# Attention in a two-layer encoder trunk: the value projection in four 256-feature passes between the q/k projections, one head per slot

## The chip, the cores and the metric

The kernel runs on one core of one Trainium2 chip. TensorE multiplies matrices into eight banks of PSUM; VectorE, ScalarE and GpSimd work on SBUF and (the first two) on PSUM; SyncE (SP) issues the loads. The engines run side by side and meet through semaphores; each takes its own instructions in the order in which they are written. The metric is the time of one execution in microseconds, lower is better.

## The reference

The trunk has two layers over 512 positions of 1024 features. Layer 0 is a gated linear attention and an MLP, layer 1 a softmax attention and an MLP; a conditioning vector scales and shifts in front of each. The change is in layer 1's attention, 16 heads of 64 features. Cut to that:

```python
def chunk_attention(u, w_in, b_in, rel_bias, w_out):
    q, k, v = jnp.split(u @ w_in + b_in, 3, axis=-1)
    ...
    # per chunk of 64 queries, over its own chunk and the 8 before it
    s = einsum('bhtd,bhjd->bhtj', qi / 8, kb) + bias
    p = softmax(where(valid, s, -1e30), axis=-1)
    o = einsum('bhtj,bhjd->bhtd', p, vb)
    ...
    return o @ w_out
```

The softmax weights of a query sum to one, so a bias that is added to every value row comes out as the same bias on every output row.

## The kernel before

All matrices are multiplied in pairs of rounded parts: an operand is split into a high part (a cast on ScalarE, the tiles `whi`, `fhi`, and index 0 of an activation tile) and a low part (operand minus high part on VectorE, `wlo`, `flo`, index 1; `lo_of`, L93), and `mm3` (L96) adds three products. A weight unit is 128 x 1024 numbers, 512 KB: a load on SP, a cast on ScalarE, a subtraction on VectorE (on GpSimd for a unit of kind "p"), then 24 products of 512 columns. The list `plan` (from L227) holds the units in the order of use, and `fill(n)` (L179) issues the next loads and splits until n units are ready. Units of kind "e" keep their two parts in the pool of activations rather than in that of weights.

Layer 1's attention is `att` (L852). Before it, the boundary has already projected q and k of pairs 0 and 1. A pair is two heads, since 128 features hold two.

- `vpass` (L968) projects the values, 512 features at a time, in four units and four PSUM banks; VectorE adds the value bias `bv` while it evicts to `vt`. Two passes run first, with scores of heads 0 and 1 between their units (L991, L992).
- Per head: `s_pre` loads a table of relative biases. `s_mm` makes transposed scores, eight products in three banks. `s_a` (L890) adds the biases on VectorE (the part beyond 256 queries is copied by ScalarE), forms maxima over the four key tiles and has GpSimd reduce them over partitions (`partition_all_reduce`, tile `mb`). `s_b1` subtracts `mb` on VectorE, `s_b2` takes exp on ScalarE. `pv` multiplies with values and with ones, so that one bank holds weighted sums and weight totals.
- Per pair: `fin1` (ScalarE: copies of the totals, Ln, Exp of minus it), `fin2` (VectorE: one Newton step, then the products), `fin3` (cast and low part of the result).
- Per q or k unit: `evac_qk` (L826) evicts with scale and bias on ScalarE (tile `f`), then casts on ScalarE (four for q, two for k) and two low parts on VectorE.

The loop `for p in range(6)` (L994) does, per turn, a q and a k unit, scores of two heads, parts of the softmax of both and of the head before, two `pv` and the division of the pair before, in an order written out by hand: `s_b1` of one head stands behind `s_a` of the next, and the ScalarE and VectorE halves of an eviction (`q_hi`, `q_lo`, `k_hi`, `k_lo`) stand apart. The last heads run in `t1` to `t5`, between parts of the first four tiles of the output projection (`ev`, L1079: (tile, k-steps)). Then comes the boundary that normalizes and opens the MLP.

Each engine's order is the order of the calls: the wrapper `InOrder` (L38) chains them.

## Time and profile before

| | us |
|---|---|
| median of 3 runs | 1256.69 (1256.31 to 1257.55) |
| the profiled execution | 1256.22 |
| its span | 1254.5 |
| TensorE busy | 1190.3 (95%) |
| VectorE busy | 884.1 (70%) |
| ScalarE busy | 523.0 (42%) |
| GpSimd busy | 263.3 (21%) |

Busy shares are means over stages with different limits. The value passes lie between about 641 and 690 us, the pair loop between 690 and 796, the last heads and the first output tiles between 796 and 856. In the order-of-time views a row is a run of like instructions: start, length, what it is, how many, and in brackets how long its engine was idle before and what ended that. PEclk is the granted clock of TensorE as a share of 2.4 GHz.

### The profile page before, as it was taken

The page shows a single profiled execution, that of the slowest core. Times are in us where ns is not written, and L with a number is a line of the kernel's source. Part 1 is how long each engine was busy: PE and PEld are TensorE (multiplying, and loading weights), DVE is VectorE, ACT ScalarE, POOL GpSimd, SP SyncE. Part 2 cuts the span into 40 slices and gives each one's busy share as a digit, 9 for nine tenths or more (in the row PEclk, how much of TensorE's full clock was granted, in tenths as well). Part 3 has the DMA queues.
Part 4 walks back from the last instruction along what each step waited for, and adds up shares of the span by engine and source line. Part 5 has one row for each costly group of instructions (what it writes and reads, how often), then busy time and mean ns, then how long its engine had stood idle before and what let it go on. Part 6 is the DMA issues. An engine that isn't in the chain of part 4 may idle for free.

```text
span 1254.5 us, 15345 instructions
## 1 busy us (share of the span) xinstructions
PE 1190.3 (95%) x5834; PEld 994.3 (79%) x5834; DVE 884.1 (70%) x1359; ACT 523.0 (42%) x816; POOL 263.3 (21%) x227
## 2 busy tenths in 40 slices
PE   8898999899999999999899999888999999999995
PEld 5676887898888888888888866667888888888885
DVE  7899889787666576567866798998875443443467
ACT  3243445366233142233483565663662331422424
POOL 4553321730000000004531221225400000000025
PEclk9998899899999999999999999998999999999998
DMA  8744634205666656654034021223055332232202
GB/s 305 269 157 152 234 101 139 97 18 178 196 188 208 189 183 201 185 168 160 8 93 136 17 67 59 68 68 118 18 171 182 96 106 89 95 101 86 99 18 67
DMA packets 48201, 159.62 MB, mean 127 GB/s; under 512 B 5440, under 2 KB 9792, under 8 KB 48128
## 3 DMA queue, kind: packets, MB, share of 16 engines
q1 hardware_dynamic: 48128, 158.66, 39.0%
q8 instruction: 45, 0.74, 0.2%
q14 instruction: 28, 0.23, 0.1%
HBM read 156.54 MB, written 2.10 MB: 126 GB/s over the span
## 4 chain that ended last, share of the span: by engine, by line
PE 54%; DVE 23%; issue 11%; ACT 6%; POOL 4%; DMA 1%; SPq 0%; ACTq 0%; DVEq 0%; POOLq 0%
PE ps L46 54%; DVE af L46 8%; DVE raw L46 3%; DVE x L46 3%; DVE ar L46 2%; ACT af L46 2%; ACT ar L46 2%; POOL af L46 1%; POOL x L46 1%; DVE wlo L46 1%; DVE u L46 1%; ACT whi L46 1%; DVE mods L46 1%; DVE d L46 1%; DMA raw<-ada 1%
## 5 line engine op out<-in xcount | busy, mean ns | idle before, releaser
L46 PE MATMUL ps<-ar,whi 128*128 128x512 f32 (+1 forms) x2816 | 806.6, 375 | 12.8 <-ACT whi L46 6.2
L46 PEld LDWEIGHTS ps<-ar,whi 128*128 128x128 f32 x2816 | 516.7, 191 | 110.1 <-ACT whi L46 9.1
L46 PE MATMUL ps<-ar,wlo 128*128 128x512 f32 (+1 forms) x1408 | 515.7, 373 | 0.5 <-DVE wlo L46 0.4
L46 PEld LDWEIGHTS ps<-ar,wlo 128*128 128x128 f32 x1408 | 268.2, 191 | 47.9 <-DVE wlo L46 2.1
L46 ACT CAST whi<-raw 128x1024 fp32r<-128x1024 f32 (+1 forms) x183 | 183.8, 1013 | 248.7 <-PE ps L46 227.6
L46 DVE TENSOR_TENSOR wlo<-raw,whi 128x1024 fp32r<-128x1024 f32 x154 | 195.5, 1274 | 26.2 <-ACT whi L46 23.8
L46 POOL TENSOR_TENSOR x<-x,af 128x512 f32<-128x512 f32 x14 | 24.7, 1792 | 633.2 <-ACT af L46 633.2
L46 DVE SCALAR_TENSOR_TENSOR x<-ps,mods,x 128x512 f32<-128x512 f32 (+1 forms) x96 | 63.1, 658 | 133.7 <-PE ps L46 133.7
L46 DVE SCALAR_TENSOR_TENSOR raw<-raw,csil 128x1024 f32<-128x1024 f32 x96 | 123.9, 1291 | 5.7 <-DMA raw<-ada 5.7
L46 DVE TENSOR_TENSOR h<-r 128x512 f32<-128x512 f32 (+1 forms) x72 | 49.3, 689 | 88.1 <-ACT r L46 86.9
L46 PE MATMUL ps<-ar,fhi 128*128 128x256 f32 (+1 forms) x448 | 93.9, 307 | 9.7 <-DVE ar L46 8.7
L46 ACT ACTIVATE r<-ps 128x512 f32<-128x512 f32 (+1 forms) x72 | 39.0, 547 | 137.1 <-PE ps L46 137.1
L46 PEld LDWEIGHTS ps<-ar,fhi 128*128 128x128 f32 x448 | 73.4, 194 | 14.2 <-DVE ar L46 10.2
L46 POOL TENSOR_TENSOR wlo<-raw,whi 128x1024 fp32r<-128x1024 f32 x22 | 60.5, 2752 | 98.9 <-ACT whi L46 93.7
L46 PE MATMUL ps<-whi,ar 128*128 128x512 f32 x256 | 80.9, 391 | 0.2 <-ACT whi L46 0.2
L46 DVE TENSOR_TENSOR ar<-h,ar 128x512 fp32r<-128x512 f32 (+1 forms) x72 | 45.6, 633 | 39.5 <-ACT ar L46 38.4
L46 PE MATMUL ps<-ar,flo 128*128 128x256 f32 (+1 forms) x224 | 67.8, 303 | 0.0
L46 ACT CAST ar<-h 128x512 fp32r<-128x512 f32 (+1 forms) x72 | 41.2, 572 | 51.9 <-DVE h L46 51.9
L46 POOL PARTITION_ALL_REDUCE mb<-af x16 | 33.2, 2077 | 133.8 <-DVE af L46 133.8
L46 PEld LDWEIGHTS ps<-whi,ar 128*128 128x128 f32 x256 | 48.1, 188 | 10.6 <-ACT whi L46 0.6
L46 PE MATMUL ps<-wlo,ar 128*128 128x512 f32 x128 | 50.1, 391 | 0.8 <-DVE wlo L46 0.8
L46 ACT ACTIVATE af<-x 128x256 f32<-128x256 f32 (+1 forms) x48 | 22.7, 486 | 56.0 <-POOL af L46 31.5
(140 smaller groups left out, 1147.3 us busy)
## 6 DMA issues: line engine op xcount, KB each, us to landing
raw<-f SPq DMA_DIRECT2D x128, 512.0 KB, 3.5
raw<-ada SPq DMA_DIRECT2D x96, 512.0 KB, 4.4
raw<-a_qk SPq DMA_DIRECT2D x16, 512.0 KB, 3.6
raw<-w_v SPq DMA_DIRECT2D x8, 512.0 KB, 4.3
raw<-w_g SPq DMA_DIRECT2D x8, 512.0 KB, 3.8
raw<-w_go SPq DMA_DIRECT2D x8, 512.0 KB, 4.6
raw<-a_v SPq DMA_DIRECT2D x8, 512.0 KB, 3.5
raw<-a_o SPq DMA_DIRECT2D x8, 512.0 KB, 3.4
```

The lines of the kernel that those rows point to most:

```text
L46: r = f(*a, **k)
```

## The change

1. The value projection becomes four passes of 256 features, two units each (`v_unit`): products of 256 columns, two PSUM banks, four 128 x 256 copies by ScalarE after the second unit. The host packs the weights accordingly (`quarter`).
2. The 20 units stand in one list, `DENSE`: v0 (two units), q2, k2, v1 (two), q3, k3, q4, k4, v2 (two), q5, k5, q6, k6, q7, k7, v3 (two). The first runs alone.
3. Heads 0 to 14 get a slot each: `s_mm`, `s_a`, the first half of the division where a pair is due, one unit, the rest of the division, `s_b`, the result's split, the unit's eviction, and `pv` of the head before (heads 0 to 11). So slot 0 has the second unit of v0, 1 q2, 2 k2 and the first of v1, 3 the second of v1, 4 q3, 5 k3 and q4, 6 k4, 7 and 8 v2, 9 q5, k5 and q6, 10 k6, 11 q7, 12 k7, 13 and 14 v3. The division of pair p is in slot 2p + 3. Head 15, `pv` of heads 12 to 15 and the last two divisions stand between parts of the output projection.
4. The value bias is no longer loaded as a 128 x 1024 tile; it lies in `col` and is added where the divided result is split (`fin3`).
5. Smaller ones: the first 128 maxima are copied by ScalarE; the division has four instructions on VectorE instead of five, three of them fused; the narrow subtraction comes before the 256-wide one; value units are all split on VectorE; two output units instead of four go to the activation pool; the table is loaded one head ahead.

```diff
-    add_units([a_v[k] for k in range(2)], kind="p")
-    add_units([a_v[k] for k in range(2, 8)])
-    for p in range(2, 8):
-        add_units([a_qk[p], a_qk[8 + p]])
+    DENSE = [("v", 0), ("q", 2), ("v", 1), ("q", 3), ("q", 4), ("v", 2), ("q", 5), ("q", 6), ("q", 7), ("v", 3)]
+    for what, i in DENSE:
+        add_units([a_v[2 * i], a_v[2 * i + 1]] if what == "v" else [a_qk[i], a_qk[8 + i]])
...
-            mx = sB[:, 1, :]
-            V.tensor_copy(mx[:, 0:P], s[0][:, 0:P])
+                if j == 0:
+                    A.copy(out=mx[:, 0:P], in_=s[0][:, 0:P])
...
             tt(V, s, s, y, ALU.mult)
-            V.tensor_scalar(out=s, in0=s, scalar1=-1.0, scalar2=2.0, op0=ALU.mult, op1=ALU.add)
-            tt(V, y, y, s, ALU.mult)
-            tt(V, s[0:64, :], pa[0:64, :], y[0:64, :], ALU.mult)
-            tt(V, s[64:128, :], pb[64:128, :], y[64:128, :], ALU.mult)
+            stt(y, s, 2.0, y, ALU.subtract, ALU.mult)
+            stt(s[0:64, :], pa[0:64, :], -1.0, y[0:64, :], ALU.mult, ALU.mult)
+            stt(s[64:128, :], pb[64:128, :], -1.0, y[64:128, :], ALU.mult, ALU.mult)
...
-            A.copy(out=r[:, 0, :], in_=s)
-            lo_of(V, r[:, 1, :], s, r[:, 0, :])
+            bv = col[:, C_BV + p:C_BV + p + 1]
+            A.activation(out=r[:, 0, :], in_=s, func=AF.Identity, bias=bv)
+            stt(r[:, 1, :], s, bv, r[:, 0, :].bitcast(F32), ALU.add, ALU.subtract)
...
+        def v_unit(n, j):
+            if j == 0:
+                vps[n] = [bank(), bank()]
+            w = next_w(False)
+            for kk in range(4):
+                k = 4 * j + kk
+                for i in range(4):
+                    mm3(vps[n][i // 2][:, (i % 2) * HT:(i % 2 + 1) * HT], uk(u, k, i * P, (i + 1) * P), wk(w, kk, HT),
+                        k == 0 and i % 2 == 0, k == KT - 1 and i % 2 == 1)
...
+            def evac():
+                for i in range(4):
...
+                    A.copy(out=ov, in_=vps[n][i // 2][:, (i % 2) * HT:(i % 2 + 1) * HT].rearrange(
...
+        def slot(i, n, pvh=None, first=True):
+            s_mm(i)
+            s_a(i)
+            if i < 15:
+                s_pre(i + 1)
+            f = todo.pop("fin", None)
+            if f is not None:
+                fin1(f)
+            ev = unit() if n else None
+            fill(2)
+            if f is not None:
+                fin2(f)
+            s_b(i)
+            if f is not None:
+                fin3(f)
+            if ev:
+                ev()
+            if pvh is not None:
+                pv(pvh)
+                if pvh % 2:
+                    todo["fin"] = pvh // 2
+            for _ in range(n - 1):
+                ev = unit()
+                fill(2)
+                ev()
...
+        more = {2: 2, 5: 2, 9: 3}
+        for i in range(15):
+            slot(i, more.get(i, 1), i - 1 if 0 < i < 13 else None)
...
+        ev = [e(lambda: s_mm(15), lambda: s_a(15), lambda: fill(2)), (0, range(5)), lambda: pv(12), (0, (5,)),
+              e(lambda: s_b(15), lambda: fill(2)), (1, range(3)), lambda: pv(13), (1, range(3, 6)),
+              e(lambda: fin1(6), lambda: fill(3), lambda: fin2(6)), (2, range(3)), lambda: pv(14), (2, range(3, 6)), lambda: fin3(6),
+              lambda: pv(15), (3, range(6)),
+              e(lambda: fin1(7), lambda: fin2(7), lambda: fin3(7)),
+              (0, (6,)), (1, (6,)), (2, (6,)), (3, (6,)),
+              (0, (7,)), (1, (7,)), (2, (7,)), (3, (7,))]
```

VectorE, from the scores of one head on. In the pair loop before (`ng` marks the score instructions of `s_a`, the last three of four here, `mb` the subtractions of `s_b1`, `ar<-f` the low parts of q or k):

```order
L46 SCALAR_TENSOR_TENSOR af_5829<-ps_5918,ng,af_5830 128x256
L46 SCALAR_TENSOR_TENSOR af_5830<-ps_5919,ng,af_5830 128x256
L46 SCALAR_TENSOR_TENSOR af_5829<-ps_5919,ng,af_5830 128x128
L46 COPY af_5830<-af_5829 128x128
L46 TENSOR_TENSOR af_5830<-af_5829 128x384
L46 TENSOR_TENSOR af_5830<-af_5830 128x256
L46 TENSOR_TENSOR af_5830<-af_5830,af_5829 128x128
L46 TENSOR_TENSOR af_5826<-af_5826,mb_5876 128x512
L46 TENSOR_TENSOR af_5826<-af_5826,mb_5876 128x384
L46 TENSOR_TENSOR af_5827<-af_5827,mb_5876 128x256
L46 TENSOR_TENSOR af_5826<-af_5826,mb_5876 128x128
L46 TENSOR_TENSOR ar_5930<-f_5928,ar_5930 64x512 x2
```

In slot 4 and the start of slot 5 after the change:

```order
L47 SCALAR_TENSOR_TENSOR af_5713<-ps_5798,ng,af_5713 128x256
L47 SCALAR_TENSOR_TENSOR af_5807<-ps_5798,ng,af_5713 128x128
L47 TENSOR_TENSOR af_5713<-af_5807 128x384
L47 TENSOR_TENSOR af_5713<-af_5713 128x256
L47 TENSOR_TENSOR af_5713<-af_5713,af_5807 128x128
L47 TENSOR_TENSOR wlo_5850<-raw_5847,whi_5849 128x1024
L47 TENSOR_TENSOR af_5807<-af_5807,mb_5818 128x512
L47 TENSOR_TENSOR af_5807<-af_5807,mb_5818 128x384
L47 TENSOR_TENSOR af_5807<-af_5807,mb_5818 128x128
L47 TENSOR_TENSOR af_5713<-af_5713,mb_5818 128x256
L47 TENSOR_TENSOR ar_5862<-f_5859,ar_5861 64x512 x2
L47 SCALAR_TENSOR_TENSOR af_5887<-ps_5876,ng,af_5820 128x256
```

Before, the subtractions behind a head's maxima are those of another head (`af_5826` against `af_5829`); after, they are those of the same head (`af_5807`), with one weight split between, and the low parts of the unit stand between them and the next head's scores.

ScalarE, one turn of the pair loop before, from the weight cast to the division (`f` is the eviction of a q or k unit, `af_6000` the division):

```order
L46 CAST whi_5882<-raw_5880 128x1024
L46 CAST ar_5859<-f_5857 64x512 x4
L46 ACTIVATE f_5928<-ps_5892,col 128x512
L46 COPY af_5829<-ps_5917 128x256
L46 COPY af_5829<-ps_5918 128x128
L46 CAST ar_5930<-f_5928 64x512 x2
L46 CAST whi_5953<-raw_5951 128x1024
L46 ACTIVATE af_5826<-af_5826 128x1024
L46 ACTIVATE af_5827<-af_5827 128x256
L46 COPY af_6000<-ps_5959 64x512
L46 COPY af_6000<-ps_5964 64x512
L46 ACTIVATE af_6000<-af_6000 128x512 x2
```

Slot 5 after the change, from the score copies on:

```order
L47 COPY af_5887<-ps_5876 128x256
L47 COPY af_5820<-af_5887 128x128
L47 COPY af_5887<-ps_5877 128x128
L47 COPY af_5902<-ps_5791 64x512
L47 COPY af_5902<-ps_5871 64x512
L47 ACTIVATE af_5902<-af_5902 128x512 x2
L47 CAST whi_5934<-raw_5932 128x1024
L47 ACTIVATE af_5887<-af_5887 128x1024
L47 ACTIVATE af_5820<-af_5820 128x256
L47 ACTIVATE ar_5948<-af_5902,col 128x512
L47 ACTIVATE f_5951<-ps_5907,col 128x512
L47 CAST ar_5953<-f_5951 64x512 x2
```

Before, eviction passes and casts stand ahead of a head's exp (the two ACTIVATE of 128x1024 and 128x256) and the division behind it; after, the division and the weight cast stand ahead of exp, and the result's split, the eviction and the casts behind it.

## Rows read from the trace of the kernel before

**Rows 1.** Busy time by stretch: pair loop (columns: us, PE, PEld, DVE, ACT, POOL, PEclk, DMA).
```profile
690.00:796.00 106.00, 98.53 (x425) 76.38 (x424) 90.61 (x173) 65.47 (x111) 25.26 (x20) 0.98 0.16 50
```

**Rows 2.** Order of time, VectorE (columns: start us, us, work, count, idle before, releaser).
```profile
652.53 2.36 DVE L46 TENSOR_TENSOR wlo<-raw,whi 128x1024 fp32r<-128x1024 f32 x2 [0.63 <-ACT whi L46]
...
716.97 1.53 DVE L46 SCALAR_TENSOR_TENSOR af<-ps,ng,af 128x256 f32<-128x256 f32 x4
...
720.37 1.79 DVE L46 TENSOR_TENSOR wlo<-raw,whi 128x1024 fp32r<-128x1024 f32 x1 [0.49 <-ACT whi L46]
...
726.35 2.54 DVE L46 TENSOR_TENSOR af<-af,mb 128x512 f32<-128x512 f32 x4
...
728.91 1.41 DVE L46 TENSOR_TENSOR ar<-f,ar 64x512 fp32r<-64x512 f32 x2
...
730.35 1.23 DVE L46 TENSOR_TENSOR wlo<-raw,whi 128x1024 fp32r<-128x1024 f32 x1
...
732.85 0.69 DVE L46 TENSOR_TENSOR af<-af 128x512 f32<-128x512 f32 x1 [1.27 <-ACT af L46]
...
736.27 1.70 DVE L46 TENSOR_TENSOR af<-af,mb 128x512 f32<-128x512 f32 x4
...
737.89 0.68 DVE L46 TENSOR_TENSOR ar<-af,ar 128x512 fp32r<-128x512 f32 x1
...
738.61 1.53 DVE L46 SCALAR_TENSOR_TENSOR af<-ps,ng,af 128x256 f32<-128x256 f32 x4
...
822.89 1.51 DVE L46 SCALAR_TENSOR_TENSOR af<-ps,ng,af 128x256 f32<-128x256 f32 x4
...
845.36 3.50 DVE L46 TENSOR_TENSOR wlo<-raw,whi 128x1024 fp32r<-128x1024 f32 x3
...
855.55 3.24 DVE L46 TENSOR_TENSOR flo<-raw,fhi 128x1024 fp32r<-128x1024 f32 x2
```

**Rows 3.** Order of time, TensorE, one turn of the loop.
```profile
702.46 4.48 PE L46 MATMUL ps<-af,vt 128*128 128x512 f32 x16
...
706.69 0.71 PE L46 MATMUL ps<-ar,whi 128*128 128x512 f32 x2
...
712.24 1.44 PE L46 MATMUL ps<-ar,ar 128*128 128x512 f32 x8
```

**Rows 4.** Order of time, ScalarE, the same period.
```profile
728.92 1.37 ACT L46 ACTIVATE af<-af 128x1024 f32<-128x1024 f32 x2 [1.99 <-DVE af L46]
...
730.31 1.18 ACT L46 COPY af<-ps 64x512 f32<-64x512 f32 x2
...
732.72 0.67 ACT L46 ACTIVATE f<-ps,bq 128x512 f32<-128x512 f32 x1
...
736.33 0.62 ACT L46 CAST ar<-af 128x512 fp32r<-128x512 f32 x1 [2.93 <-DVE af L46]
...
739.12 0.66 ACT L46 COPY af<-ps 128x256 f32<-128x256 f32 x2 [2.17 <-DVE af L46]
...
740.94 1.03 ACT L46 CAST whi<-raw 128x1024 fp32r<-128x1024 f32 x1
...
741.88 2.53 ACT L46 CAST ar<-f 64x512 fp32r<-64x512 f32 x4
```

**Rows 5.** Order of time, GpSimd, the same period.
```profile
720.05 1.78 POOL L46 PARTITION_ALL_REDUCE mb<-af  x1 [11.87 <-DVE af L46]
...
726.52 2.15 POOL L46 PARTITION_ALL_REDUCE mb<-af  x1 [4.69 <-DVE af L46]
```

**Rows 6.** A wait of TensorE, and busy time by stretch around it (granted clock: third from last).
```profile
773.02 1.63 PE L46 MATMUL ps<-ar,ar 128*128 128x512 f32 x8 [2.25 <-DVE ar L46]
...
772.00:776.00 4.00, 2.98 (x12) 2.62 (x13) 2.75 (x4) 3.70 (x7) 1.04 (x2) 0.79 0.04 9
...
776.00:780.00 4.00, 4.00 (x15) 3.18 (x15) 3.65 (x6) 1.12 (x3) 0.00 (x0) 0.79 0.41 122
...
780.00:784.00 4.00, 4.00 (x20) 3.04 (x19) 3.97 (x11) 1.75 (x5) 0.00 (x0) 1.00 0.00 0
```

More of the change, by code (lines that the diff above doesn't have):

```diff
@@ L33 @@
 C_BK = 180
-N_COL = 188
+C_BV = 188
+N_COL = 196
 SH1, SC1, G1, SH2, SC2, G2 = range(6)
@@ L58, in trunk @@
 @with_exitstack
-def trunk(ctx, tc, xT, c, ada, cols, gk1, gk2, w_qk, w_v, w_g, w_go, a_qk, a_v, a_bv, a_tab,
+def trunk(ctx, tc, xT, c, ada, cols, gk1, gk2, w_qk, w_v, w_g, w_go, a_qk, a_v, a_tab,
           a_win, a_o, f1, f2, out):
@@ L210, in add_out @@
         for i, u in enumerate(units):
-            plan.append(("e" if early and i < 4 else "p" if i < pool else "w", u))
+            plan.append(("e" if early and 1 < i < 4 else "p" if i < pool else "w", u))
             if fgs and not early and 1 < i < 6:
@@ L982, in both @@
-        def both(*fs):
+        vps = {}
+        def v_unit(n, j):
[7 more added lines that the diff above has]
+                        k == 0 and i % 2 == 0, k == KT - 1 and i % 2 == 1)
+            if j == 0:
+                return lambda: None
+            def evac():
+                for i in range(4):
+                    ov = vt[i][:, 2 * n:2 * n + 2, :].rearrange("p a (b c) -> p a b c", c=64)[:, :, 0:3:2, :]
+                    A.copy(out=ov, in_=vps[n][i // 2][:, (i % 2) * HT:(i % 2 + 1) * HT].rearrange(
+                        "p (a b c) -> p a b c", b=2, c=64))
+            return evac
@@ new lines, in qk_unit, with evac, unit @@
+        def qk_unit(p, is_k):
+            ps = mtile(u, False)
+            def evac():
+                for f in evac_qk(p, is_k, ps):
+                    f()
+            return evac
+        dense = []
+        for what, i in DENSE:
+            for j in range(2):
+                dense.append((v_unit if what == "v" else qk_unit, i, j))
+        def unit():
+            f, i, j = dense.pop(0)
+            fill(1)
+            return f(i, j)
+        todo = {}
+        def slot(i, n, pvh=None, first=True):
[23 more added lines that the diff above has]
+                ev()
@@ L983, in f, with e @@
+        s_pre(0)
+        fill(2)
+        unit()()
+        fill(2)
+        more = {2: 2, 5: 2, 9: 3}
+        for i in range(15):
+            slot(i, more.get(i, 1), i - 1 if 0 < i < 13 else None)
+        def e(*fs):
             def f():
@@ L1153, in half, with quarter @@
         return w.reshape(4, 2, P, 2, S).transpose(3, 0, 2, 1, 4).reshape(8, P, 2 * S)
+    def quarter(w):
+        return w.reshape(2, 4, P, 4, HT).transpose(3, 0, 2, 1, 4).reshape(8, P, 4 * HT)
     colsT = lambda v: v.reshape(-1, P).T
@@ L1174 @@
         "a_qk": mt(aw[:, :2 * D]),
-        "a_v": half(aw[:, 2 * D:]),
-        "a_bv": a["att_b_in"][:, 2 * D:],
+        "a_v": quarter(aw[:, 2 * D:]),
         "a_tab": tab[:, 256][None, :],
```

130 lines of the change are left out of this document (12 added, 118 removed).

## The prediction

> **What bounds the kernel now.** I read the page's busy shares first, then the stretches by engine, then VectorE, ScalarE and GpSimd in order of time through one period of the pair loop, and last TensorE. TensorE is nearly always busy over the whole program, but not in the part that the change rewrites: in the pair loop it works 98.5 of 106 us, VectorE 90.6, ScalarE 65.5 [rows 1]. So no engine is full there. In order of time one finds why: one period is 716.97 to 738.61, 21.64 us for two heads and two projection units [rows 2]. TensorE needs 5.55 us for a unit (706.69 to 712.24), 1.44 for the scores of a head and 4.23 for two heads' weighted sums (702.46 to 706.69), so 2 x 5.55 + 2 x 1.44 + 4.23 = 18.2 [rows 3]. The remaining 3.4 us are a chain that goes back and forth between VectorE and ScalarE, each waiting for the other in its written order: ScalarE is idle 1.99 and 2.17 us for VectorE, VectorE 0.49 and 1.27 for ScalarE [rows 2, 4]. The pair loop hides one thing well: the all-reduce of one head's maxima on GpSimd (1.78 to 2.15 us, [rows 5]) runs while VectorE does another head's work. What a rewrite of this loop is worth is therefore read from its longest in-order chain, not from busy time.
>
> **The change, part by part.** Durations are of one execution of 1256.2 us (span 1254.5, 1.7 around it), 0.5 under the median of the runs; the sum is made against 1256.2.
>
> *Fewer or moved instructions.* The copy of the first 128 maxima leaves VectorE for ScalarE, the division loses one VectorE instruction per pair, the eight evictions of the values leave VectorE for sixteen on ScalarE, two lower halves of value weights come from GpSimd to VectorE. That is some 8 us less of VectorE work. None of it counts by itself; it counts where it stands in a chain below. The value products have half as many columns each and twice the number; I price a value unit like any unit (same columns), bounded above by twice that, and neither reaches the sum, since TensorE is not what a slot waits for.
>
> *The chain of a head without a division (even slots).* VectorE's new order is: scores of head i, one lower half of weights, the four subtractions of head i, the lower halves of the unit's q or k, scores of head i+1. ScalarE's is: score copies, weight cast, exp of head i, bias pass of the unit, casts. Both are strict, so from one head's first score instruction to the next:
> - scores, hand-over and all-reduce: 716.97 to 720.05 + 1.78 = 4.86, less 0.1 for the copy that left, 4.8 with the hop [rows 2, 5]. Before, another head's subtractions lay here; now only one 1.23 us weight instruction does, inside it.
> - subtractions until exp may start: four take 1.70 when GpSimd is quiet (2.54 beside an all-reduce, 726.35); the last, narrower one is not waited for: 1.3.
> - exp 1.4, bias pass 0.7, first cast 0.6 (a quarter of 2.53), two lower halves 1.4 [rows 2, 4].
>
> Sum 10.2 us with a k unit; with a q unit the second lower half waits for the third cast, 10.8. TensorE's own work in that slot is 5.55 + 1.44 + 2.1 = 9.1, so the chain decides.
>
> *The chain of a head with a division (odd slots from 3).* ScalarE: three score copies 1.0 (the second waits for VectorE's first score instruction), the four division steps 730.31 to 732.85 = 2.5, weight cast 1.0. VectorE's weight instruction stands before the division and waits for that cast, though nothing in the division needs it: 1.2. Then division 2.9 (732.85 to 736.27 = 3.4, less the instruction that goes, 0.5), subtractions 1.3, exp 1.4, cast of the result 0.6, bias pass 0.7, cast 0.6, lower halves 1.4. Sum 14.6 with k, 15.2 with q [rows 2, 4].
>
> *Slots with a value unit.* The eviction is ScalarE's, four copies, estimated at 0.35 each from the 0.66 of two score copies [rows 4]. Odd: the chain ends with the result's lower half, 1.0 + 2.5 + 1.0 + 1.2 + 2.9 + 1.3 + 1.4 + 0.6 + 0.7 = 12.6. Even: VectorE is free early, but the next head's maxima wait for ScalarE's copies, which stand behind exp (ends at 7.5) and eviction (8.9); that makes 8.4.
>
> *Slots with more units.* Each further q or k unit adds a weight cast 1.0, a bias pass 0.7 and its casts behind the last ones on ScalarE, then a lower half. Slot 2: the k casts end at 9.4, weight cast 1.0, VectorE's part 1.2, 11.6. Slot 5: k casts end at 13.8, then 1.0 + 0.7 + three q casts 1.9 + 0.7 = 18.1. Slot 9: q casts end at 15.1, the k unit's at 15.1 + 1.0 + 0.7 + 1.3 = 18.1, then 1.0 + 0.7 + 1.9 + 0.7 = 22.4.
>
> *Sum to the last head's scores.* Slots 6, 10, 12 (k): 30.6. 1, 4 (q): 21.6. 2: 11.6. 0, 8, 14 (value): 25.2. 3, 7, 13 (value, odd): 37.8. 11: 15.2. 5: 18.1. 9: 22.4. Together 182.5, and 0.1 per slot for hand-overs, 184. The start is earlier than before: slot 0 comes after one value unit and not after three. Its first score instruction follows the first weight instruction of 652.53 [rows 2], with two ScalarE passes more ahead of it: 654.5, between 653 and 656. So the scores of head 15 come at 654.5 + 184 = 838.5; before, at 822.89 [rows 2]: 15.6 us late.
>
> *The end of the stage.* From there TensorE sets the pace: four weighted sums (8.5) and 27 of the 32 k-steps of the first four output tiles at 0.69 = 18.7, so 27.2. It starts when the last value eviction is done, about 0.5 after the scores. The update of the fourth tile follows 0.9 later: 838.5 + 0.5 + 27.2 + 0.9 = 867.1. Before it ended at 855.55: 11.5 late. Then three weight instructions stand on VectorE (row of 845.36: 3.50) that before had been done in front of the tile updates, and the next row, the lower halves of 855.55, comes after them: the boundary's VectorE chain shifts by 3.5 more [rows 2]. Total +15, 1256.2 + 15 = 1271.
>
> *Hidden costs.* The 512 KB broadcast load of the value bias goes, the small columns grow; both lie under transfers nobody waits for. The two output weights that leave the activation pool free space there only. Loads of score tables now stand one head ahead of their use between the weight loads on SP; a slot of 10 us covers them, and what is queued behind, a weight load, has five buffers. I price both at 0, up to +3 if a slot's table arrives late.
>
> *A price that could come on top.* TensorE will wait in every slot, for score banks or exp. After its wait of 2.25 us at 773.02 the granted clock of 772 to 780 was 0.79, 1.2 GHz for some of it [rows 6]: 8 x 0.21 = 1.7 us lost. In the slots this is hidden (a unit is ready some 10 us before its bias pass). On the path are slots 2 and 9 and the start of the end stage. The Trainium skill (TensorE: Matmul & The Clock Gate, "A second HAM failure mode: psum-queue depth-cycling") describes such small waits between groups as a lasting loss through falling and rising clock; by it every wait costs, while the pair loop here, with several such waits, kept a mean of 0.98 [rows 1]. I take 0 for the clock in the sum and give it a case of its own below.
>
> **Rivals.**
> - *Faster: the slots overlap and cost only their busiest engine.* For: VectorE loses work and the value pass, where it was idle, is spread over all heads. Slot by slot the larger of TensorE's and VectorE's own work sums to about 157 instead of 184, the stage ends 27 us earlier than I say: 1244. It decides if the mean slot is under about 11.2 us instead of 12.3 (15 us over 15 slots is 1 us each). Against: the next head's scores stand behind this unit's lower halves on VectorE, and those behind exp on ScalarE; nothing lets them pass.
> - *No change: chains 1 us a slot shorter than the rows say.* Would need each all-reduce almost hidden; 1256.
> - *The clock stays low.* Four falls on the path (slots 2 and 9, the start and a second wait in the end stage) at 1.7 each: 1271 + 7 = 1278; if half of the 27.2 us of the end stage ran at 1.2 GHz, 1285. For: a wait in each slot, and the fall after the one of 773.02. Against: full clock in 780 to 784 right after the fall [rows 6].
>
> **How the numbers follow.** Forecast (chains as summed, 1262 to 1280): 0.68, time 1271. Clock: 0.16. Faster: 0.11. No change: 0.05. About 0.2% (2.5 us) is what a measurement of this kernel can tell from none. So faster 0.11, same 0.05, slower 0.84. The range leaves out the faster case and the far end of the clock: 1257 to 1285. Its width: each chain is uncertain by 0.4 us a slot, 6 in all; the value unit, tables and first start by 3 each way; the clock by +7.
>
> **What would show it.** Right: in order of time VectorE idles about 2 us before the subtractions in the slots with no division, with the all-reduce as releaser or nothing but GpSimd running, and about 1.8 us before the weight instruction in the others, released by ScalarE's weight cast; even slots of 10 to 11 us, odd ones of 12 to 15; TensorE's busy share from 650 to 840 under 88%; the chain of waits there holds VectorE, ScalarE and GpSimd and almost no TensorE; the scores of head 15 at about 838. Wrong: slots near 9 us; TensorE on the chain inside the slots; a slot waiting for a table or a weight load; or a boundary after the stage that is no later than the stage itself.

## The result: 30 us slower, twice the forecast

The changed kernel takes 1286.76 us (median of 4 runs, 1285.19 to 1287.07), the kernel before 1256.83 beside it: ratio 1.0235, 95% interval 1.0218 to 1.0253. 1271 was forecast, 1257 to 1285 as range. The direction was right, the size half of what came; the profiled execution took 1287.07.

**The stretch as a whole.** Busy time by stretch of the kernel after, columns as in [rows 1]:

```profile
690.00:796.00 106.00, 89.11 (x427) 72.25 (x426) 69.93 (x129) 59.13 (x106) 21.65 (x16) 0.94 0.20 69
650.00:840.00 190.00, 160.06 (x834) 133.11 (x833) 123.78 (x234) 106.14 (x191) 37.90 (x31) 0.94 0.20 64
```

Every engine is busy for less of the same 106 us than before: TensorE 89 for 98.5, VectorE 70 for 90.6. Much the same work is spread over more time, which fits a chain of waits; the row alone does not show one. TensorE's share from 650 to 840 is 84%. The chain that ended last can be followed back to 795.45, and from there to 846.66 it holds work of VectorE, ScalarE and GpSimd and none of TensorE.

**One even and one odd slot.** Order of time on VectorE, head 6 (731.39) and head 7 (742.50), then head 8 (the rows that [rows 2] show of before from 716.97 to 738.61):

```profile
731.39 1.53 DVE L47 SCALAR_TENSOR_TENSOR af<-ps,ng,af 128x256 f32<-128x256 f32 x4
...
734.08 1.22 DVE L47 TENSOR_TENSOR wlo<-raw,whi 128x1024 fp32r<-128x1024 f32 x1
736.98 1.70 DVE L47 TENSOR_TENSOR af<-af,mb 128x512 f32<-128x512 f32 x4 [1.68 <-POOL mb L47]
741.06 1.41 DVE L47 TENSOR_TENSOR ar<-f,ar 64x512 fp32r<-64x512 f32 x2 [2.38 <-ACT ar L47]
742.50 1.53 DVE L47 SCALAR_TENSOR_TENSOR af<-ps,ng,af 128x256 f32<-128x256 f32 x4
...
747.37 1.23 DVE L47 TENSOR_TENSOR wlo<-raw,whi 128x1024 fp32r<-128x1024 f32 x1 [2.09 <-ACT whi L47]
...
754.78 0.75 DVE L47 SCALAR_TENSOR_TENSOR ar<-af,col,ar 128x512 fp32r<-128x512 f32 x1 [1.71 <-ACT ar L47]
```

The waits named ahead are all there: for the all-reduce (1.68), for the cast behind the exponentials (2.38), for the weight cast ahead of the division (2.09), for the result's cast (1.71). ScalarE in the even slot, and GpSimd's all-reduces of both heads (compare [rows 4, 5]):

```profile
738.44 1.37 ACT L47 ACTIVATE af<-af 128x1024 f32<-128x1024 f32 x2 [4.71 <-DVE af L47]
739.71 0.67 ACT L47 ACTIVATE f<-ps,col 128x512 f32<-128x512 f32 x1
740.41 1.26 ACT L47 CAST ar<-f 64x512 fp32r<-64x512 f32 x2
```
```profile
734.36 2.58 POOL L47 PARTITION_ALL_REDUCE mb<-af  x1 [15.56 <-DVE af L47]
745.44 1.78 POOL L47 PARTITION_ALL_REDUCE mb<-af  x1 [8.50 <-DVE af L47]
```

ScalarE idles 4.71 us and then does three things in a row, of which only the last two are awaited by VectorE. The unit's products had been complete since 735.5, when TensorE ended its last matmul of them. The all-reduce takes 2.58 in the even slot, beside a weight subtraction of VectorE that began 0.28 ahead of it (734.08), and 1.78 in the odd one, where VectorE waits.

**The first head.** GpSimd around slot 0:

```profile
650.71 1.93 POOL L47 MEMSET vt<- 128x512 f32 x4 [18.73 <-DVE ar L47]
652.98 0.70 POOL L47 TENSOR_SCALAR ng<-tab_c 128x16 f32<-128x16 f32 x1 [0.34 <-DMA tab_c<-a_tab]
660.29 1.80 POOL L47 PARTITION_ALL_REDUCE mb<-af  x1 [6.60 <-issue]
```

VectorE's maxima of head 0 were done at 656.5; the all-reduce starts 3.8 us later, behind 6.60 us in which GpSimd waits for nothing that the profile shows. Before, 9.73 us lay between the sign change and the first all-reduce, so that such a start could lie in them unseen.

**The end of the stage.** VectorE from the updates of the output tiles to the shift, and ScalarE beside it:

```profile
875.53 1.40 DVE L47 SCALAR_TENSOR_TENSOR x<-ps,mods,x 128x512 f32<-128x512 f32 x2
876.85 3.48 DVE L47 TENSOR_TENSOR wlo<-raw,whi 128x1024 fp32r<-128x1024 f32 x3
880.25 2.35 DVE L47 TENSOR_TENSOR flo<-raw,fhi 128x1024 fp32r<-128x1024 f32 x2
885.88 6.52 DVE L47 TENSOR_TENSOR x<-x,af 128x512 f32<-128x512 f32 x4 [3.28 <-ACT af L47]
```
```profile
881.62 1.05 ACT L47 CAST fhi<-raw 128x1024 fp32r<-128x1024 f32 x1 [4.50 <-DMA raw<-f]
884.31 1.05 ACT L47 CAST fhi<-raw 128x1024 fp32r<-128x1024 f32 x1 [1.64 <-DMA raw<-f]
885.27 0.57 ACT L47 COPY af<-ps 128x512 f32<-128x512 f32 x1
```

The three weight subtractions that were forecast to come late do (3.48), and something more: ScalarE's copy of the shift (885.27) stands behind two casts that wait for loads, and VectorE waits 3.28 for it. TensorE at the start of the end stage, and where it pays for the late shift:

```profile
846.66 3.62 PE L47 MATMUL ps<-af,vt 128*128 128x512 f32 x6 [2.48 <-ACT vt L47]
...
900.73 2.26 PE L47 MATMUL ps<-af,ones_c 128*128 128x256 f32 x4 [8.96 <-DVE af L47]
```

The slots of the changed kernel and of three experiments below, from one head's first score instruction on VectorE to the next, in us:

| slot (its eviction) | forecast | after | exponentials last | three misses out | best |
|---|---|---|---|---|---|
| 0 (value) | 8.4 | 10.0 | 10.9 | 7.5 | 6.6 |
| 1 (q) | 10.8 | 12.6 | 8.5 | 11.2 | 8.5 |
| 2 (k, and half a value unit) | 11.6 | 11.9 | 12.8 | 11.7 | 10.1 |
| 3, 7, 13 (division, no q or k) | 12.6 each | 13.0, 13.1, 13.1 | 11.2 each | 13.0, 13.1, 13.1 | 10.3, 10.2, 11.2 |
| 4 (q) | 10.8 | 11.7 | 8.6 | 10.9 | 8.6 |
| 5 (division, k, q) | 18.1 | 18.5 | 17.1 | 18.5 | 16.5 |
| 6, 10, 12 (k) | 10.2 each | 11.1 each | 8.8, 8.8, 9.3 | 10.3 each | 8.8 each |
| 8, 14 (value) | 8.4 each | 7.2 each | 7.2 each | 7.5, 7.2 | 7.2 each |
| 9 (division, q, k, q) | 22.4 | 24.3 | 21.8 | 23.1 | 20.9 |
| 11 (division, q) | 15.2 | 15.6 | 12.7 | 15.6 | 11.6 |
| sum, with hand-overs | 184 | 191.4 | 167.1 | 183.4 | 155.1 |
| head 0's scores | 654.5 | 653.7 | 651.9 | 653.5 | 653.5 |
| head 15's scores | 838.5 | 845.1 | 818.9 | 837.0 | 808.6 |
| time (median) | 1271 | 1286.8 | 1258.3 | 1274.4 | 1244.3 |

### The profile page after: what moved, and what is told of

It reads as the page before. It is cut to its first block, busy times and chain, and to the rows that moved or that the text cites. A ratio compares the mean times of both kernels' runs of the same rounds, so it can differ in the third digit from the quotient of the medians.

```text
span 1285.3 us, 15741 instructions
## 1 busy us (share of the span) xinstructions
PE 1196.3 (93%) x6026; PEld 1007.8 (78%) x6026; DVE 864.2 (67%) x1329; ACT 530.7 (41%) x848; POOL 260.0 (20%) x225
## 5 line engine op out<-in xcount | busy, mean ns | idle before, releaser
L47 PE MATMUL ps<-ar,whi 128*128 128x512 f32 (+1 forms) x2848 | 816.6, 375 | 18.4 <-ACT whi L47 6.3
L47 PEld LDWEIGHTS ps<-ar,whi 128*128 128x128 f32 x2848 | 522.5, 191 | 117.9 <-ACT whi L47 9.2
L47 PE MATMUL ps<-ar,wlo 128*128 128x512 f32 (+1 forms) x1424 | 521.4, 373 | 0.2 <-DVE wlo L47 0.2
L47 PE MATMUL ps<-ar,fhi 128*128 128x256 f32 (+1 forms) x416 | 82.8, 298 | 7.6 <-DVE ar L47 7.5
L47 PE MATMUL ps<-whi,ar 128*128 128x256 f32 (+1 forms) x384 | 88.7, 321 | 0.0
L47 PEld LDWEIGHTS ps<-ar,fhi 128*128 128x128 f32 x416 | 67.5, 195 | 10.1 <-DVE ar L47 8.5
L47 PEld LDWEIGHTS ps<-whi,ar 128*128 128x128 f32 x384 | 65.1, 192 | 5.1
L47 ACT ACTIVATE af<-af 128x1024 f32<-128x1024 f32 (+2 forms) x48 | 31.9, 697 | 78.4 <-DVE af L47 77.8
L47 PE MATMUL ps<-wlo,ar 128*128 128x256 f32 (+1 forms) x192 | 61.5, 320 | 0.0
L47 PE MATMUL ps<-ar,flo 128*128 128x256 f32 (+1 forms) x208 | 61.3, 295 | 0.0
```

The costliest lines, as they stand in the source:

```text
L47: r = f(*a, **k)
```

## The experiments

Theory: the in-order chain VectorE, GpSimd, VectorE, ScalarE, VectorE of a slot sets its length, with some terms sized too small, and a boundary cost more. Rivals: TensorE's work and its clock hold the slots and the waits lie beside that; or the loss is all behind the stage.

### 1. The exponentials last on ScalarE

```
-            s_b(i)                  # four subtractions, two exponentials
+            s_b(i)                  # four subtractions
             if f is not None: fin3(f)
             if ev: ev()
+            s_e(i)                  # the two exponentials
```

> The changed kernel with one move: in each of the 15 slots the two exponentials of the scores stand behind the unit's eviction and the division's last cast on ScalarE, not ahead of them; VectorE's order is kept. Theory 1 (the end of the slots is set by the chain over ScalarE, so the waits of VectorE for ScalarE's casts are the loss): the 2.38 us wait ahead of the eviction's low halves goes in the six even slots with a q or k unit, most of the 1.71 us wait ahead of the division's low half in the odd ones; the slots shrink by 20 to 27 us together, head 15's scores come at 818 to 826 instead of 845, and the time falls by 18 to 25 us, to 1262 to 1269. Theory 2 (the slots are held by TensorE's work and its clock, and the waits of VectorE lie beside it): 0 to -4 us. Theory 3 (the exponentials, late on ScalarE, hold up the next head's copies by their 1.36 us): -5 to -10.

Measured: 1258.29, 28.5 less than the changed kernel; against the kernel before the ratio is 1.0013 (1.0003 to 1.0022). The slots shrink by 24.3 together, inside theory 1's 20 to 27, and head 15's scores come at 818.9 (1.9 of the difference was there at head 0, which no edit touches); the time fell by more than the 18 to 25 expected. VectorE, head 6's slot, and ScalarE in it:

```profile
720.86 1.53 DVE L47 SCALAR_TENSOR_TENSOR af<-ps,ng,af 128x256 f32<-128x256 f32 x4
...
726.45 1.70 DVE L47 TENSOR_TENSOR af<-af,mb 128x512 f32<-128x512 f32 x4 [1.68 <-POOL mb L47]
728.18 1.41 DVE L47 TENSOR_TENSOR ar<-f,ar 64x512 fp32r<-64x512 f32 x2
729.62 1.52 DVE L47 SCALAR_TENSOR_TENSOR af<-ps,ng,af 128x256 f32<-128x256 f32 x4
```
```profile
723.08 0.69 ACT L47 ACTIVATE f<-ps,col 128x512 f32<-128x512 f32 x1
723.80 1.26 ACT L47 CAST ar<-f 64x512 fp32r<-64x512 f32 x2
727.85 1.36 ACT L47 ACTIVATE af<-af 128x1024 f32<-128x1024 f32 x2 [2.78 <-DVE af L47]
```

The eviction now fills ScalarE's idle time, the 2.38 us wait is gone and nothing takes its place; the slot falls from 11.11 to 8.76. No instruction was added or removed on any engine, so in the changed kernel TensorE's work did not set the slots. Theory 3 falls too: in head 7's slot it is ScalarE that waits for VectorE before its first score copy, 0.9 us, and not the other way.

### 2. The output weights split early, as before

```
-    "e" if early and 1 < i < 4 else ...
+    "e" if early and i < 4 else ...
-    e(lambda: fin1(7), lambda: fin2(7), lambda: fin3(7)),
+    e(lambda: fin1(7), lambda: fin2(7), lambda: fill(4), lambda: fin3(7)),
```

> The changed kernel with the output projection's weights as before in two respects: all of its first four units are split into the activation pool (the changed kernel: units 2 and 3 only), and the last units are called for before the last head pair's low half is computed, not behind the four tile updates. Theory 1 (some 6 us of the 30 are lost behind the end stage, where ScalarE's copy of the shift stands behind weight casts that wait for a late load): the shift subtractions come 2 to 3 us behind the fourth tile update, as before, not 9; the time falls by 5 to 8 us, to 1279 to 1282, and head 15's scores stay at 845. Theory 2 (that wait has cover, and what follows is held by the slots alone): 0 to -2.

Measured: 1282.27, 4.5 less, a little under theory 1's 5 to 8 and above theory 2; head 15's scores are at 844.5. VectorE, the same place:

```profile
880.11 4.32 DVE L47 TENSOR_TENSOR flo<-raw,fhi 128x1024 fp32r<-128x1024 f32 x2
884.35 4.78 DVE L47 TENSOR_TENSOR x<-x,af 128x512 f32<-128x512 f32 x6
```

The wait for the shift is gone. Its subtractions start only 1.5 earlier than in the changed kernel, for the tile updates, which now have the three weight subtractions ahead of them, end 3.3 later (880.11 against 876.85), and the two subtractions of 2.35 took 4.32. But what follows the shift's six subtractions starts 4.5 earlier (889.06 against 893.52): they take 4.7 and not 7.6. Of these 4.5, 0.6 was there at head 0 already. So the order at the boundary cost some 4, and by far most of the 30 lies in the slots.

### 3. Without the all-reduce

```
-            G.partition_all_reduce(mb, mx, P, bass_isa.ReduceOp.max)
+            mb = mx
```

> The changed kernel without GpSimd's all-reduce: the column maximum of each partition is subtracted as it is (left out: the maximum over the 128 partitions). Theory 1 (in even slots the all-reduce is on the chain, in odd ones it lies under the division): VectorE's wait of 1.7 to 2.0 us ahead of the four subtractions goes in the seven even slots, and 3.5 us in slot 0; odd slots keep their length within 0.5 us; 13 to 18 us less, 1269 to 1274. Theory 2 (TensorE holds the slots): 0 to -4. Theory 3 (the four subtractions are slow because GpSimd's reads press on them): they fall from 1.70 us and odd slots shorten as well; more than -18.

Measured: 1268.68, 18.1 less. Slots 4, 6, 8, 10, 12 and 14 lose 1.75 to 1.78 each, slot 0 loses 3.6, and slot 2 and the odd slots 0.1 or less (13.07 stays 13.07). That is theory 1's pattern, but for slot 2: in even slots the all-reduce is on the chain, in odd ones it lies under the division. In slots 1 and 2 of the changed kernel the weight subtraction waits 1.0 for its cast and then ends after the all-reduce, which is why nothing is gained there. The slots are 14.5 shorter together; head 0 was 1.9 earlier, as in experiment 1, and the rest came behind head 15.

### 4. The weight subtraction behind the scores' subtractions

```
+            state["defer"] = []      # collect VectorE's low halves
             fill(2)
             if f is not None: fin2(f)
             s_b(i)
+            for x in state["defer"]: x()
```

> The changed kernel with VectorE's low half of the weight unit moved behind the four subtractions in each slot (the cast on ScalarE stays where it is). Theory 1 (the low half stretches the all-reduce from 1.78 to 2.58 us in even slots, and its wait of 2.09 us for the cast stands ahead of the division in odd slots): even slots lose 0.8 to 1 us each, since 1.2 us of it now lie in the wait for the eviction, odd slots with a division 1 to 2 us; 10 to 18 us less, 1269 to 1277. Theory 2 (TensorE holds the slots, or the all-reduce takes 2.58 us for another reason): 0 to -5; the all-reduce stays at 2.5 us.

Measured: 1268.82, 17.9 less, the upper end of theory 1. GpSimd and VectorE, head 6:

```profile
728.28 1.78 POOL L47 PARTITION_ALL_REDUCE mb<-af  x1 [13.47 <-DVE af L47]
```
```profile
730.10 1.70 DVE L47 TENSOR_TENSOR af<-af,mb 128x512 f32<-128x512 f32 x4 [2.01 <-POOL mb L47]
731.72 1.22 DVE L47 TENSOR_TENSOR wlo<-raw,whi 128x1024 fp32r<-128x1024 f32 x1
734.18 1.40 DVE L47 TENSOR_TENSOR ar<-f,ar 64x512 fp32r<-64x512 f32 x2 [1.25 <-ACT ar L47]
```

All 16 all-reduces take 1.78 to 1.80. So the 0.80 us of stretch in an even slot is the price of that one subtraction beside it, paid by GpSimd alone: the subtraction takes 1.22 in both places. Moved, it costs nothing in the later even slots with q or k, since it lies in what was the wait for ScalarE. Slots 4, 6, 10 and 12 fall by 0.8, the dividing ones by 2.1 (slot 9 by 3.2); slots 0, 8 and 14, without that wait, grow by 1.2, 0.3 and 0.3.

### 5. Three edits together

Experiments 1 and 2, and number 4 in the dividing slots alone:

```
+            state["defer"] = [] if f is not None else None
             fill(2)
...
+            for x in state["defer"] or []: x()
```

> The changed kernel with three edits together: the exponentials last on ScalarE in each slot, the output projection's first four units split early with the last ones called for ahead of the last pair's low half, and VectorE's low half of the weight unit behind the four subtractions in the odd slots that divide (in even slots it stays beside the all-reduce). Against the kernel with the exponentials last alone (1258.3 us, head 15's scores at 818.9). Theory 1 (the chain over VectorE still sets the slots): the six dividing slots lose about 1 us each and the boundary 4.6, so 1247 to 1249. Theory 2 (with the exponentials last TensorE has become the bound of the slots: it was busy 37.4 of 40 us there against 33.5): the edit in the odd slots is worth 0 to 2 us together, and the time is 1252 to 1254.

Measured: 1249.91, ratio to before 0.9942 (0.9928 to 0.9955). Between the two theories: 8.4 less than experiment 1 alone. Five of the six dividing slots lost 0.6 to 1.2 each, as theory 1 had it, slot 13 none; head 15's scores come 5.4 earlier, and 3.0 came behind them, not 4.6. On TensorE, from head 2's scores to head 15's, experiment 1 takes 140.7 us with waits in between (667.95 to 808.67); here it takes 135.1 (668.20 to 803.34) and waits for nothing. So theory 2 was right in part: much of this stretch is TensorE's now (experiment 7), but only once the edit in the dividing slots had been made.

### 6. The first all-reduce, taken early

```
+        G.partition_all_reduce(wr, ones_c[:, 0:64], P, bass_isa.ReduceOp.max)
         ac = es.enter_context(tc.tile_pool(name="ac", bufs=1))
```

> The changed kernel with the one extra all-reduce ahead of the attention's set-up and nothing else. Theory 1 (the first all-reduce's late start is 3 us of slot 0 on a chain that nothing absorbs): the first real all-reduce begins within 0.3 us of its maxima, slot 0 shrinks from 10.0 us by 2 to 3.5, and the time falls by 2 to 3.5 us. Theory 2 (what slot 0 loses is given back in slots 1 and 2, which wait for the passes over x on ScalarE): 0 to -1.

> The kernel of the three edits with one all-reduce more, over 64 columns and without use, issued on GpSimd ahead of the attention's set-up. Theory 1 (the first all-reduce after other GpSimd work begins 6.6 us behind the last of it, whatever its input waits for, and slot 0 pays what of that sticks out): the extra one takes that start-up while nothing waits, the wait in slot 0 goes, 1.5 to 3 us less than the kernel of the three edits. Theory 2 (the small operation on the table behind it brings the start-up back): no change, the first real one still starts 6 us or more behind it.

Both got slower, against both theories of the first run: 1290.44 on the changed kernel (+3.7), 1254.28 on the three edits (+4.4). GpSimd in the second:

```profile
636.69 0.54 POOL L47 PARTITION_ALL_REDUCE wr<-ones_c  x1 [5.87 <-issue]
649.23 1.92 POOL L47 MEMSET vt<- 128x512 f32 x4 [12.00 <-DVE ar L47]
657.97 0.29 POOL L47 TENSOR_SCALAR ng<-tab_c 128x16 f32<-128x16 f32 x1 [6.82 <-issue]
664.12 1.80 POOL L47 PARTITION_ALL_REDUCE mb<-af  x1 [5.86 <-DVE wlo L47]
```

Three waits of 5.9 to 6.8 us with no work in them: into the all-reduce, out of it for the sign change of a 128x16 table, and in again. Head 0's scores need that table and began 4.8 later. Theory 2 of the second run named the mechanism and missed its price. The next run moves the sign change to VectorE:

```
-        G.tensor_scalar(out=ng, in0=tab_c, scalar1=-1.0, ...
+        V.tensor_scalar(out=ng, in0=tab_c, scalar1=-1.0, ...
```

> The kernel of the three edits with the unused all-reduce ahead of the attention's set-up, and the table's sign change (128x16) on VectorE, not on GpSimd behind it. In the run without that move the sign change itself began 6.8 us late and the first real all-reduce another 5.9 us behind it. Theory 1 (GpSimd pays 6 to 7 us each time it goes from its ordinary operations to the all-reduce or back; memory sets don't count): the first real all-reduce begins within 0.3 us of its maxima, slot 0 falls from 9.9 to 6.5 to 8 us, and the time is 1.5 to 3.5 us under the kernel of the three edits (1249.9). Theory 2 (the memory sets of the value tiles bring the start-up back as well): 0 to +4.

```profile
637.03 0.54 POOL L47 PARTITION_ALL_REDUCE wr<-ones_c  x1 [5.82 <-issue]
649.57 1.92 POOL L47 MEMSET vt<- 128x512 f32 x4 [12.00 <-DVE ar L47]
656.45 1.78 POOL L47 PARTITION_ALL_REDUCE mb<-af  x1 [4.96 <-DVE af L47]
```

Measured: 1244.32, ratio to before 0.9898 (0.9883 to 0.9913), the fastest kernel of this study: 5.6 under the three edits, more than the 1.5 to 3.5 expected. The first real all-reduce follows its maxima in 0.2 us, slot 0 takes 6.6, and slot 2 lost another 1.7. TensorE's scores of head 2 come at 663.23, 5.0 earlier, and those of head 15 at 798.38, again 135.1 us later: the gain was made ahead of head 2.

### 7. Is TensorE the bound now?

The three edits without the all-reduce:

```
-            G.partition_all_reduce(mb, mx, P, bass_isa.ReduceOp.max)
+            mb = mx
```

> The kernel of the three edits without GpSimd's all-reduce (left out: the maximum over the 128 partitions). Theory 1 (in the kernel of the three edits TensorE sets the slots, 38 of 40 us busy, and the chain over GpSimd lies beside it): VectorE's waits move elsewhere and the slots keep their length but for slot 0; 0 to 4 us less than 1249.9. Theory 2 (the chain over GpSimd still sets the even slots): seven times 1.7 us and slot 0 less, 12 to 16 us, as in the changed kernel, where leaving it out gave 18.

Measured: 1238.25, 11.7 less than the three edits, just under theory 2's 12 to 16 and far from theory 1's 0 to 4. On VectorE, slots 6, 10, 12 and 14 lost 1.8 each, slot 2 1.6 and slot 0 3.5; but slots 4 and 8 kept their length, and slot 9 grew by 1.8. Busy time by stretch in the kernel of the three edits (the other shows 40.00 as well, of 207 matmuls):

```profile
690.00:730.00 40.00, 40.00 (x199) 32.68 (x198) 32.79 (x63) 28.00 (x52) 9.03 (x7) 1.00 0.25 79
```

TensorE's scores of head 2 and head 15, the three edits first, then without the all-reduce:

```profile
668.20 1.54 PE L47 MATMUL ps<-ar,ar 128*128 128x512 f32 x8
...
803.34 1.45 PE L47 MATMUL ps<-ar,ar 128*128 128x512 f32 x8
807.30 0.72 PE L47 MATMUL ps<-ar,fhi 128*128 128x512 f32 x2 [2.51 <-ACT af L47]
```
```profile
662.50 1.54 PE L47 MATMUL ps<-ar,ar 128*128 128x512 f32 x8
...
797.65 1.45 PE L47 MATMUL ps<-ar,ar 128*128 128x512 f32 x8
```

Between the two TensorE waits for nothing in either kernel, and it takes the same 135.1 us: shorter slots on VectorE gave it nothing there. For this stretch theory 1 is right.

The gain lies at the two ends. Ahead of head 2's scores are 5.7, 0.5 of it there at head 0 already, where a wait of 3.36 (664.33, for ScalarE) is gone. Behind head 15's are 6.3 of the profiled executions, where waits of 2.51, 0.89 and 0.53 are gone, and with them a stretch at a granted clock of 0.57 (808 to 812; 1.00 without the all-reduce).

The chain that ended last shows the same: with the all-reduce it runs over TensorE from 664.33 for 98.4 us, and behind that over VectorE, ScalarE and GpSimd, with three all-reduces of 2.6 and one of 1.8 on it; without, it stays on TensorE from 644.99 for 175.1. So the full row of 690 to 730 did mean that TensorE was the bound, while between 763 and 800 the row is as full (10.00 in every 10 us) and the chain runs elsewhere. What told them apart is the time between the same two instructions in two kernels.

### 8. The small edits alone, in the kernel before

```
-            V.tensor_copy(mx[:, 0:P], s[0][:, 0:P])
+            A.copy(out=mx[:, 0:P], in_=s[0][:, 0:P])
...
-            V.tensor_scalar(out=s, in0=s, scalar1=-1.0, scalar2=2.0, op0=ALU.mult, op1=ALU.add)
-            tt(V, y, y, s, ALU.mult)
+            stt(y, s, 2.0, y, ALU.subtract, ALU.mult)
```

> The kernel before with two of the change's small edits alone: the division's separate 2 - x pass folded into its product (8 instructions of 0.43 us fewer on VectorE) and the 128-column start of the maxima copied on ScalarE (16 of 0.22 us fewer on VectorE, as many more on ScalarE). Theory 1 (in the kernel before VectorE's chain sets the second half of the slots): 3 to 5 us less, 1252 to 1254. Theory 2 (these passes lie beside TensorE's work, or the copies delay ScalarE's weight casts): within 1.5 us of no change.

Measured: 1252.86, ratio 0.9966 (0.9954 to 0.9978): 4.5 less, theory 1. The period of two heads falls from 21.64 to 20.95. So what the change took off VectorE was worth 4.5 where two heads alternate; if that carries over, the rest of the change cost some 34.

### 9. The three misses taken out

The changed kernel with the forecast's own order of ScalarE, the low half deferred in even slots only, the early all-reduce with the sign change on VectorE, and experiment 2:

```
+            state["defer"] = [] if f is None else None
...
+        G.partition_all_reduce(wr, ones_c[:, 0:64], P, bass_isa.ReduceOp.max)
...
+        V.tensor_scalar(out=ng, in0=tab_c, scalar1=-1.0, ...
...
+    "e" if early and i < 4 else ...
```

> The changed kernel without the three costs that the forecast had left out, and with the order of the exponentials as the change has it: the weight unit's low half behind the subtractions in the slots that do not divide (so the all-reduce there takes 1.78 us and not 2.58), the first all-reduce's start-up taken ahead of the attention, and the output projection's first four units split early. Theory 1 (the forecast's chain is right and these three are what it missed): the even slots from 4 on take 10.3 us instead of 11.1, slot 0 falls by 3, odd dividing slots stay at 13 us, the boundary gives 4.6; head 15's scores come at 836 to 838 (838.5 was forecast) and the time is 1271 to 1275, beside the forecast's 1271. Theory 2 (the rest was lost to TensorE's clock, which is low at 724 to 728 and 784 to 788 us, whatever the slots take): 1279 to 1283.

Measured: 1274.37, ratio to before 1.0139 (1.0122 to 1.0156), inside theory 1's 1271 to 1275. VectorE at head 15:

```profile
836.95 1.52 DVE L47 SCALAR_TENSOR_TENSOR af<-ps,ng,af 128x256 f32<-128x256 f32 x4
```

Forecast was 838.5. With these three gone the sum of the slots is 183.4 where 184 was forecast: the chain was the right one, and these were most of what it lacked. That the sum agrees better than single slots do (7.5 and 7.2 for 8.4 in 8 and 14, 23.1 for 22.4 in 9) is luck in part: of the 8.0 that the slots lost, 2.5 came in slots 1 and 9, where none of the three costs stood. Slots 3, 5, 7, 11 and 13, where nothing was edited, keep their length to 0.02.

### 10. Which of the two is stretched

The fastest kernel, with two memory sets between the maxima and the weight subtraction of the later slots that do not divide:

```
+            if f is None and i > 2:
+                V.memset(win[i][:, 0, HT:S], 0.0)
+                V.memset(win[i][:, 0, HT:HT + P], 0.0)
             fill(2)
```

> The fastest kernel so far (1244.3 us) with two memory sets on VectorE (128x256 and 128x128 over a table that is no longer read, together some 0.4 us) between the maxima and the weight subtraction of the six later slots without a division, so that the weight subtraction begins behind the start of the all-reduce and not 0.28 us ahead of it. Theory 1 (of a two-input VectorE instruction and an all-reduce the one that starts first keeps its length and the other is stretched, as 720.05 with 720.37 and 734.08 with 734.36 have it): the all-reduce falls from 2.58 to 1.78 us, the subtraction rises from 1.22 to 1.6 to 1.8, the slots lose 0.4 to 0.8 us each, and the time falls by 2 to 4.5 us, to 1240 to 1242. Theory 2 (the all-reduce is stretched by the subtraction whatever starts first, or by any VectorE work beside it): it stays at 2.5 us or more, and the added instructions cost 0 to 2.4 us, 1244 to 1247.

GpSimd and VectorE in head 6's slot:

```profile
717.08 1.78 POOL L47 PARTITION_ALL_REDUCE mb<-af  x1 [13.13 <-DVE af L47]
```
```profile
716.89 0.53 DVE L47 MEMSET af<- 128x256 f32 x2
717.34 1.86 DVE L47 TENSOR_TENSOR wlo<-raw,whi 128x1024 fp32r<-128x1024 f32 x1
719.12 1.69 DVE L47 TENSOR_TENSOR af<-af,mb 128x512 f32<-128x512 f32 x4
```

Theory 1 holds for the lengths: all 16 all-reduces take 1.78, the six subtractions 1.86 or 1.87, and VectorE no longer waits ahead of the four subtractions. The slots lose 0.6 each (slot 4 0.1). The time does not follow: 1244.08, ratio to before 0.9895 (0.9879 to 0.9912), as the kernel without the sets. Slot 9 gave 1.2 back (20.9 to 22.1; ScalarE now waits up to 2.2 us for TensorE's products there, 1.0 without the sets). Head 15's scores come 1.7 earlier on VectorE, but on TensorE they stand at 798.42, for 798.38 without the sets, and the shift's subtractions start at 846.4 for 845.9. TensorE holds here, as in experiment 7.

## Why the prediction was right in kind and wrong in size

The mechanism held: in-order chains over VectorE, ScalarE and GpSimd set the slots. What failed is the size of terms in the sum. The all-reduce was put at 1.78 with a weight instruction beside it for nothing, and took 2.58 in six slots; GpSimd's start of 6.6 before its first all-reduce was not in the sum; the boundary was put at +3.5 and came to +9.6. With these three taken out, the last as far as experiment 2 does it, experiment 9 measured 1274.4 for a forecast of 1271.

- *No engine is full; read the longest in-order chain.* Right. Moving two ScalarE instructions per slot, with no work changed, gave back 28.5 of 30 us, some 2 of it already there at head 0.
- *Even slot 10.2 with k, 10.8 with q.* The steps stand in the trace as listed. Mis-sized is the all-reduce, 1.78 from [rows 5], with a weight instruction of 1.23 said to lie "inside it" at no cost. It measured 2.58 in all even slots from 4 on, and those with q or k are 0.9 longer than summed. The row at 720.05 did have a weight instruction beside it, which began 0.3 later and took 1.79 [rows 2]: the later one pays. In the new order the weight instruction begins first, and the all-reduce pays, on the chain. The trace of before had that case too, unread: at 814.20 an all-reduce of 2.69 behind a subtraction of 1.22 at 814.02.
- *Odd slots 12.6 and 15.2.* 13.0 to 13.1 and 15.6: 0.4 too short each, no single cause shown. The price of the weight instruction ahead of the division is confirmed by experiment 4 (2.1 a slot).
- *Slots 0 and 1, 8.4 and 10.8.* 10.0 and 12.6. GpSimd's start of 6.6 us was not in the sum, since before it lay in an idle stretch of 9.73. The way back did show in the trace of before: its first ordinary operation behind the last all-reduce, at 835.72, stands behind 6.72 us of nothing. Also, ScalarE's passes over x, 1.5 in each of slots 0 to 2, were counted for the start only. Value slots 8 and 14 were 1.2 too long.
- *Sum of slots and start.* 845.1 for 838.5: 6.6 of the 15.8 by which the forecast fell short of this execution.
- *End of the stage, 28.6 from head 15's scores to the fourth update.* 31.7 (876.85 less 845.14), 3.1 more. TensorE began at 846.66 after a wait of 2.48, 1.5 behind the scores where 0.5 was allowed, and the clock was down in the stretch that follows:

```profile
844.00:848.00 4.00, 1.52 (x3) 0.83 (x3) 2.66 (x8) 3.01 (x9) 0.00 (x0) 0.77 0.19 77
848.00:852.00 4.00, 4.00 (x15) 2.65 (x15) 1.82 (x4) 0.07 (x1) 1.79 (x1) 0.81 0.00 0
```

  The granted clock of 0.77 and 0.81 means 1.2 GHz for part of each; lost are 4 x 0.23 + 4 x 0.19 = 1.7 us, the unit price that the prediction gave one fall. This is the place it named. In experiment 1, where the end stage comes 26 us earlier, 812 to 816 shows 0.59 behind a wait of 2.51, so that fall was not won back there.
- *Boundary +3.5.* The step with the largest relative miss. Before, 3.17 us lay from the fourth update to the shift's subtractions (855.55 to 858.72), after 9.03 (876.85 to 885.88): 5.9 more, not 3.5. From there to the end it takes 3.7 longer than before (401.2 against 397.5): 1.8 of it lies in the shift's six subtractions (7.6 for 5.8), and the rest comes behind TensorE's wait of 8.96 and was not traced further. The prediction saw the late weight instructions and did not ask what their late buffers hold up: the loads of the next stage's weights, ScalarE's casts of them, and behind those in written order the copy of the shift. The chain that ended last shows it: two of the late weight subtractions (876.85), a load of `raw` (879.22), a cast (884.31), the copy, the shift's subtractions. "The two output weights that leave the activation pool free space there only" is the sentence that was wrong. Experiment 2 gave 4.5 back, 0.6 of it at head 0.
- *The account.* 6.6 in slots and start, 3.1 in the end stage, 2.4 and 3.7 at the boundary: 15.8, which is 1287.1 less 1271.3 (1256.2, 11.5 and 3.5 before rounding).
- *The clock as a rival.* TensorE was at 1.2 GHz in 724 to 728 and 784 to 788 (0.50, after waits of 8.55 and 4.94), late in slots 5 and 9. The chain that ended last holds no TensorE work from 795.45 to 846.66, though 824 to 828 shows 0.71, so the clock did not set the last slots; slots 6 and 10, ahead of that, are as long as 12 (11.1). Slots 5 and 9 have falls in experiment 9 too (0.50 in 720 to 724, 0.57 in 776 to 780), so whether they would be shorter without them is not shown.
- *The rival "faster".* It was priced at 1244 and set to decide at a mean slot of 11.2 us. The changed kernel's mean is 12.8. With the exponentials last it is 11.1 and the time equals before; with all edits it is 10.3 and 1244.3. The threshold was good; what stood between was the order on one engine, as the prediction's "against" said. The rival's condition is met in that kernel too: TensorE, the busiest engine, waits for nothing from head 2's scores to head 15's.

## What to carry to other kernels

When work is spread over slots on in-order engines, write down for each engine what stands ahead of the instruction that another engine awaits: here one ScalarE pair that nobody needed at once, placed ahead of one that VectorE needed, cost 28 of 1287 us. Size a shared step from a row with the neighbour, and the order of starting, that it will have. A buffer released late is charged to whatever is queued behind the load that it holds up, so follow each moved release through the load, the cast and the next instruction on that engine. And ask after each gain whether the bound has moved: compare the time between the same two instructions of the busiest engine in both kernels.

## What the runs showed of the hardware that was not expected

- GpSimd's start into the first all-reduce takes 5.6 to 7.4 us over these runs, and the way back to an ordinary operation 6.7 to 7.6; without the all-reduce neither is there (experiments 3 and 7). Memory sets cost no such start: one follows an all-reduce by 0.06 us (670.06 in the changed kernel), and an all-reduce follows one after 4.96 us, 0.2 behind its maxima (656.45 in the fastest kernel). The Trainium skill (GPSIMD Engine Reference, "2.1 Instruction dispatch") gives about 6 us for the first call of a freshly loaded kernel, without an instruction in the profile; the trace agrees in size, with 5.82 and 6.60, and shows that such a wait is paid again in each direction. That these waits are such loads is not shown.
- Of an all-reduce and one two-input VectorE instruction over 1024 columns the one that starts first keeps its length, and the other is stretched: 2.58 for 1.78 behind it, or 1.86 for 1.22. Four shorter subtractions that began 0.17 ahead of an all-reduce were stretched, and the all-reduce too: 2.54 for 1.70 and 2.15 for 1.78 [rows 2, 5]. The Trainium skill (GPSIMD Engine Reference, "1. Specifications") says that the two engines share their SBUF interfaces, with contention when a VectorE instruction has two inputs there; the trace agrees, and only the rows tell who pays, and how much.
- TensorE's busy row was full (10.00 of 10 us) through a stretch in which the chain that ended last first ran over TensorE and then over other engines (experiment 7): a full row does not tell the two apart.
